# Second parts of plain FFN weight chunks by an accumulating transfer, an earlier read of the plain gate, and tile 4 as a Strassen pair

## The chip, the cores and the metric

The kernel runs on one core of one Trainium2 chip. Its time is the device time of one launch in microseconds (us). Before the change it is 1909.13 us, the median of three runs (1908.13 to 1910.99).

The engines are named as the profile names them: PE is the matrix engine (PEld its weight loads), DVE the vector engine, ACT the scalar engine, POOL the engine that issues software transfers here, and SP the engine that issues the weight loads.

## The reference

One inference step of a two-layer hybrid decoder trunk, in float32. All 520 columns (512 prompt positions and 8 samples) pass through each layer:

```python
x = x + 0.5 * swiglu_ffn(rms_norm(x, p['ffn1_norm']), p['ffn1_wg'], p['ffn1_wu'], p['ffn1_wd'])
h = rms_norm(x, p['mix_norm'])
z = h @ p['w_in']            # retention, sliding-window attention, conv module
...
x = x + y                    # y = concat(three mixers) @ w_out
x = x + 0.5 * swiglu_ffn(rms_norm(x, p['ffn2_norm']), p['ffn2_wg'], p['ffn2_wu'], p['ffn2_wd'])

def swiglu_ffn(x, wg, wu, wd):
    return (jax.nn.silu(x @ wg) * (x @ wu)) @ wd
```

The model width is 1024 and the hidden width of an FFN 2816, that is 22 hidden tiles of 128. There are four FFNs (two per layer) and two mixers. The change touches the FFNs.

## The kernel before

**Precision.** x lies transposed in the core's memory, 128 rows by 520 columns in 8 pieces. Every float32 product is made of three matmuls on float32r operands: each operand is split into a rounded first part and the rest, and first x second, first x first and second x first are summed in PSUM (`mm3`, L342; `product`, L334). For a weight the first part is a cast on ACT (L290, in `split_hi`) and the second part a subtraction on DVE, `wl = w - wh` (L296, in `split_lo`). One matmul works on 128 x 260 columns.

**The weight stream.** All weights come in one order as chunks of 128 x 1024 (512 KB), loaded by SP (L245) into 4 raw buffers. A chunk's buffer is loaded anew when its splits are issued (`done`). The stream is used in one of two ways. A *plain* chunk is split as a whole (one cast and one subtraction of 128 x 1024) and feeds 48 matmuls. Two chunks can instead feed seven *products* of Strassen's kind (a11, s1, s2, a12, s3, s4, a22 in this order), each with a 128 x 512 operand and 12 matmuls; the operands s1, s2 and s4 are sums of weight blocks, made by four DVE additions (L258, L260, L261, L263). So a plain hidden tile takes 2 x 48 = 96 matmuls and a paired one 84, with more work on DVE. The list `PAIRED` names the paired hidden tiles. The hidden results go into three groups (tiles 0 to 7, 8 to 15, 16 to 21); the steps d0, d1 and d2 multiply each group by the down weights, d0 after tile 8, d1 after tile 16 and d2 last. d0 and d1 are paired (`pair_down`), d2 is plain.

**The order of the work.** Each engine runs its instructions in the order in which the program is written. `ahead` splits the weights up to 6 slots ahead of the one in use (a plain chunk counts two slots, a product one). It is called where a chunk or product begins: casts first, then the subtractions, and for a product the next sums. The elementwise work of the tiles before (`gated`, `sum_parts`, `two_parts` and the like) waits in a list from which `advance` takes one step after every product or second k.

**PSUM.** A plain hidden tile has a gate buffer `og` and an up buffer `ou`. After both are complete DVE reads them (`t = og * R`, L443, and `u = ou * R`, L444). A paired tile or pair of down tiles (`seven`) has the buffers `one`, `mid` and the half `c22`. The pool holds four buffers that go round, and so the `mid` of a pair after a plain tile lies where that tile's `og` was: its second product, s1, can begin only after L443. The third product, s2, adds into `c22`, into which ACT first copies the product a11 (L518). A pair that follows a pair waits likewise for the reads of the pair before (`late`, L556 and L557, and `last`, L561, in `pair_hidden`; L542 in `pair_down`). `silu` is L428 on ACT, its product with `u` is L430 on DVE.

Of the kernel before, what the change touches and what calls it, by code (L numbers as in the profile page):

```python
# [10 lines left out]
F32 = mybir.dt.float32  # L11
F32R = mybir.dt.float32r
AF = mybir.ActivationFunctionType
ALU = mybir.AluOpType
# [3 lines left out]
KD = D // 128  # L18
NT = SEQ + NB
HN = NT // 2  # L20
FFN = 2816
NF = FFN // 128

PAIRED = (5, 6, 7, 9, 10, 11, 13, 14, 15, 17, 18, 20, 21)


GROUPS = ((0, 8, True), (8, 16, True), (16, 22, False))
# [82 lines left out]
def ffn_steps():  # L110


    steps = [("hidden", f) for f in range(NF)]
    for n, g in reversed(list(enumerate(GROUPS))):
        steps.insert(min(g[1] + 1, NF), ("down", n))
    return steps


def ffn_tiles(first, gate, up):


    return [(o, k) for k in range(KD) for o in (gate, up)] if first else [(o, k) for o in (gate, up) for k in range(KD)]


def streams():

    w_in = [n for i, n in enumerate(ORDER) if len(n) == 3 and n[:2].isupper() and n not in ORDER[:i]]
    w_out = [(r, int(n[1])) for i, n in enumerate(ORDER) if n[0] in OUT and n[1:].isdigit() and n not in ORDER[:i] for r in OUT[n[0]]]
    return w_in, w_out


MIX_CHUNKS = (len(streams()[0]) * KD + len(streams()[1])) // CT
RAW = 4


@with_exitstack
def step_kernel(ctx: ExitStack, tc: tile.TileContext, io: dict):
    nc = tc.nc

    def pool(name, bufs, **kw):  # L140
        return ctx.enter_context(tc.tile_pool(name=name, bufs=bufs, **kw))

    const = pool("const", 1)
    wraw = pool("wraw", RAW)
    wspl = pool("wspl", 3)
# [11 lines left out]
    R = const.tile([128, NT], F32, name="R")  # L157
# [26 lines left out]
    def v2(t):  # L184
        return t.rearrange("p (a b) -> p a b", a=2)
# [9 lines left out]
    def wt(name, n=NT, dt=F32, bufs=None):  # L195
        return work.tile([128, n], dt, tag="t", name=name)

    def ptile():
        return psum.tile([128, 2, 512], F32, tag="o", name="o")
# [4 lines left out]
    seq, slot = [], [0]  # L204
# [7 lines left out]
    def add_products(n):  # L212
        for _ in range(n):
            for name in PRODUCTS:
                seq.append((name, chunk[0]))
                slot.append(slot[-1] + 1)
            chunk[0] += 2

    chunk = [0]
    for _ in range(DEPTH):  # L220
        for part in range(3):
# [3 lines left out]
            for step, n in ffn_steps():  # L225
                if step == "hidden" and n in PAIRED:
                    add_products(1)
# [4 lines left out]
                else:  # L232
                    add_chunks((GROUPS[n][1] - GROUPS[n][0]) * KD // CT)
    assert chunk[0] == NCH
    raw, done, spl, ready = {}, set(), {}, set()
    at, nxt, loaded, pending = [0, 0], [0], [0], []

    def load(dma=True):

        while loaded[0] < NCH and (loaded[0] < RAW or loaded[0] - RAW in done):  # L240
            i = loaded[0]
            loaded[0] += 1
            raw[i] = wraw.tile([128, CT * 128], F32, tag="w", name="w")
            if dma:
                nc.sync.dma_start(raw[i], io["w"][i])  # L245

    def sums(u):

        if u >= len(seq) or u in ready:
            return  # L250
        ready.add(u)
        name, i = seq[u]
        if name == "chunk":
            return
        load()
        (a21, a11), (a22, a12) = ((raw[j][:, :PC], raw[j][:, PC:]) for j in (i, i + 1))
        if name == "s1":
            nc.vector.tensor_add(Rd[:, 0, :PC], a21, a22)  # L258
        elif name == "s2":
            nc.vector.tensor_sub(a21, a21, a11)  # L260
            nc.vector.tensor_add(Rd[:, 1, :PC], a21, a22)  # L261
        elif name == "s4":
            nc.vector.tensor_sub(Rd[:, 0, :PC], a12, Rd[:, 1, :PC])  # L263

    def source(u):
        name, i = seq[u]
        if name == "chunk":
            return raw[i]
        if name[0] == "a":
            return dict(a11=raw[i][:, PC:], a12=raw[i + 1][:, PC:], a22=raw[i + 1][:, :PC])[name]  # L270
        return raw[i][:, :PC] if name == "s3" else Rd[:, int(name == "s2"), :PC]

    def parts_of(u):

        tag = ("wh", "wl")
        if seq[u][0] == "chunk":
            return tuple(wspl.tile([128, CT * 128], F32R, tag=t, name=t) for t in tag)
        t = tag[slot[u] % 2]
        w = wspl.tile([128, CT * 128], F32R, tag=t, name=t)
        return w[:, :PC], w[:, PC:]  # L280

    def split_hi():

        u = nxt[0]
        if u < len(seq):
            nxt[0] += 1
            load()
            sums(u)
            spl[u] = parts_of(u)
            nc.scalar.copy(spl[u][0], source(u))  # L290
            pending.append(u)

    def split_lo(n=9):
        for u in pending[:n]:
            h, lo = spl[u]
            nc.vector.tensor_sub(lo, source(u), h.bitcast(F32))  # L296
            name, i = seq[u]
            if name in ("chunk", "s3", "a22"):
                done.add(i + (name == "a22"))
                load()  # L300
        del pending[:n]

    def ahead(u):

        old = len(pending)
        while nxt[0] < len(seq) and slot[nxt[0] + 1] - slot[u] <= 6:
            split_hi()
        if seq[u][0] == "chunk":
            split_lo()
        else:  # L310
            split_lo(old)
            sums(nxt[0])
            sums(nxt[0] + 1)

    def next_tile(look=True):
        u, c = at
        if c == 0 and look:
            ahead(u)
        at[:] = (u, c + 1) if c + 1 < CT else (u + 1, 0)
        s = slice(c * 128, (c + 1) * 128)  # L320
        return spl[u][0][:, s], spl[u][1][:, s]
# [17 lines left out]
    def mm3(o, w, vh, vl, first, last):  # L339
        for i, (a, b) in enumerate(((w[0], vl), (w[0], vh), (w[1], vh))):  # L340
            for s in range(2):
                nc.tensor.matmul(  # L342
                    o[:, s, :HN], lhsT=a, rhs=b[:, s * HN : (s + 1) * HN],
                    start=first and i == 0, stop=last and i == 2,
                )
# [20 lines left out]
    def run(parts):  # L366
        for _ in parts:
            pass
# [45 lines left out]
    def advance():  # L414
        while waiting:
            try:
                next(waiting[0])
                return True
            except StopIteration:
                del waiting[0]  # L420

    def flush():
        while advance():
            pass
# [8 lines left out]
    def hidden(norm, first):  # L433

        og, ou = ptile(), ptile()
        for i, (o, k) in enumerate(ffn_tiles(first, og, ou)):
            mm3(o, next_tile(), xh[:, k], xl[:, k], k == 0, k == KD - 1)
            if i % 2:
                advance()
        if first:  # L440
            run(norm)
        t, u = wt("t"), wt("u")
        nc.vector.tensor_mul(v2(t), og[:, :, :HN], v2(R))  # L443
        nc.vector.tensor_mul(v2(u), ou[:, :, :HN], v2(R))  # L444
        return t, u

# [104 lines left out]
    def pair_hidden(blocks):  # L551
        t, u, v = wt("t"), wt("u"), wt("v")[:, :HN]

        def late(c12, c22, m5):
            for d, c in ((t, c12), (u, c22)):
                nc.vector.tensor_add(d[:, HN:], c, v)  # L556
                nc.vector.tensor_mul(d[:, HN:], d[:, HN:], R[:, HN:])  # L557

        def last(one):
            for i, d in enumerate((t, u)):  # L560
                nc.vector.tensor_mul(d[:, :HN], one[:, i, :HN], R[:, :HN])  # L561

        seven(blocks, late, last, lambda m5: nc.scalar.copy(v, m5))
        return t, u

    def ffn(l, name, norm, after):
        hs, even, spare, xs = {n: [] for n in range(len(GROUPS))}, None, [], []
        for step, n in ffn_steps():
            if step == "hidden":
                g = next(i for i, (a, b, _) in enumerate(GROUPS) if a <= n < b)  # L570
                t, u = pair_hidden(xs) if n in PAIRED else hidden(norm, n == 0)
                flush()
                waiting.append(gated(t, u))
                if GROUPS[g][2] and n % 2:
                    waiting.append(pair_blocks(even, u, spare, hs[g]))
                elif GROUPS[g][2] or n == GROUPS[g][0]:
                    even = u
                else:
                    waiting.append(two_parts(u, hs[g]))
                waiting.extend(input_sums(l, name, j, xs) for j in {0: (0,), 1: (1, 2), 2: (3,)}.get(n, ()))  # L580
                continue
# [20 lines left out]
    def mix(l, after):  # L602
# [586 lines left out]
        def chunk_hi():  # L1189
            while True:  # L1190
                split_hi()
                yield

        def chunk_lo():
            while True:
                split_lo(1)
                yield
# [98 lines left out]
def host_arrays(i):  # L1296
# [17 lines left out]
    for t, j in zip(gu, (1, 2)):  # L1314
# [3 lines left out]
        for step, n in ffn_steps():  # L1318
            if step == "hidden":
                g = t[:, n]  # L1320
                if n in PAIRED:

# [96 lines left out]
```

## Time and profile before

| What | Before |
|---|---|
| Median of the runs | 1909.13 us (1908.13 to 1910.99) |
| The profiled execution | 1916.64 us, its span 1914.9 us |
| PE busy | 1843.5 us (96%) |
| DVE busy | 1565.0 us (82%) |
| ACT busy | 991.9 us (52%) |
| POOL busy | 23.3 us (1%) |
| DMA | 189.35 MB, mean 99 GB/s |

The profiled execution is 1.74 us longer than its span, and 7.5 us longer than the median run. A line of the timeline gives the start, the duration, the engine, the line of the kernel, the operation with its operands (out<-in) and its shape; in square brackets stands how long the engine was idle before it and what it waited for. A line of the view of waits gives the engine and line that waited, what it waited for, the sum, the number of times and the longest. A line of the windows gives the stretch, its length, and each engine's busy time with the number of its instructions.

### The profile page before, as it was taken

The numbers are of one execution on the slowest core, as the hardware profiler recorded it, in microseconds if no ns is written. First come the engines' busy times: TensorE is split into PE (matmuls) and PEld (weight loads), VectorE is DVE, ScalarE is ACT, GpSimd is POOL, SyncE is SP. The second block draws the span as 40 slices with busy tenths as digits, with TensorE's granted clock in tenths as the row PEclk, the third lists the DMA queues.
The fourth block names the chain that finished last, engine by engine and source line by source line (L and its number), as shares of the span: only waits on it lengthen the run. The fifth ranks groups of instructions, "written<-read, shape, count | busy, mean of one in ns | idle before, by whom it ended". The sixth has DMA issues, their size and how long they took to land.

```text
span 1914.9 us, 37060 instructions
## 1 busy us (share of the span) xinstructions
PE 1843.5 (96%) x15182; PEld 1818.6 (95%) x15182; DVE 1565.0 (82%) x2691; ACT 991.9 (52%) x1844; POOL 23.3 (1%) x52
## 2 busy tenths in 40 slices
PE   8999999999989999999999999999998999999998
PEld 8999999999989999999999999999998999999998
DVE  8988898688667989888778988976886579889984
ACT  6545555433765645545455455545237555455452
POOL 0000000000100000000000000000000000000000
PEclk9999999999999999999999999999999999999999
DMA  5233333433313222333333332434332132333332
GB/s 181 77 101 100 89 100 111 138 108 114 117 35 97 79 89 89 90 110 98 112 88 90 91 97 89 123 110 127 100 114 102 45 98 69 100 107 92 93 96 89
DMA packets 54170, 189.35 MB, mean 99 GB/s; under 512 B 6272, under 2 KB 7152, under 8 KB 54000
## 3 DMA queue, kind: packets, MB, share of 16 engines
q1 hardware_dynamic: 50784, 177.35, 30.4%
q0 software_dynamic: 3072, 9.53, 1.5%
q8 instruction: 119, 1.95, 0.4%
q14 instruction: 51, 0.42, 0.1%
q10 hardware_dynamic: 144, 0.11, 0.0%
HBM read 179.50 MB, written 7.45 MB: 98 GB/s over the span
## 4 chain that ended last, share of the span: by engine, by line
PE 61%; DVE 26%; ACT 5%; DMA 4%; issue 4%; SPq 0%; DVEq 0%; ACTq 0%; POOL 0%; POOLq 0%
PE o L342 32%; PE o L334 27%; DVE wl L296 5%; DMA w<-in_w 3%; DVE wh L296 3%; DVE m L474 2%; DVE u L430 2%; DVE m L502 1%; DVE w L260 1%; DVE Rd L263 1%; ACT t L428 1%; DVE t L557 1%; DVE t L556 1%; DVE t L561 1%; DVE u L556 1%
## 5 line engine op out<-in xcount | busy, mean ns | idle before, releaser
L342 PE MATMUL o<-xl,wh 128*128 128x260 f32 x1920 | 389.3, 284 | 6.6 <-DVE xl L387 6.1
L342 PE MATMUL o<-xh,wl 128*128 128x260 f32 x1920 | 387.1, 283 | 1.1 <-DVE wl L296 1.1
L342 PE MATMUL o<-xh,wh 128*128 128x260 f32 x1920 | 386.9, 283 | 0.0
L334 PE MATMUL o<-m,wh 128*128 128x260 f32 x2592 | 350.5, 285 | 23.0 <-DVE t L443 11.3
L334 PE MATMUL o<-m,wl 128*128 128x260 f32 x2592 | 351.7, 285 | 21.3 <-DVE t L443 9.8
L290 ACT CAST wh<-w 128x1024 fp32r<-128x1024 f32 (+1 forms) x318 | 261.1, 821 | 200.8 <-PE o L342 127.7
L334 PEld LDWEIGHTS o<-m,wh 128*128 128x128 f32 x2592 | 327.4, 189 | 27.3 <-issue 12.3
L334 PEld LDWEIGHTS o<-m,wl 128*128 128x128 f32 x2592 | 328.5, 190 | 25.7 <-issue 10.8
L342 PEld LDWEIGHTS o<-xl,wh 128*128 128x128 f32 x1920 | 296.9, 189 | 7.9 <-ACT wh L355 6.1
L342 PEld LDWEIGHTS o<-xh,wl 128*128 128x128 f32 x1920 | 296.6, 189 | 1.3 <-DVE wl L296 1.3
L342 PEld LDWEIGHTS o<-xh,wh 128*128 128x128 f32 x1920 | 296.1, 189 | 0.0
L296 DVE TENSOR_TENSOR wl<-w,wh 128x1024 fp32r<-128x1024 f32 x150 | 183.3, 1222 | 36.1 <-ACT wh L290 32.7
L342 PE MATMUL o<-m,wh 128*128 128x260 f32 x1024 | 164.5, 282 | 4.1 <-DVE m L510 4.1
L342 PEld LDWEIGHTS o<-m,wh 128*128 128x128 f32 x1024 | 140.0, 188 | 5.0 <-DVE m L510 5.0
L290 ACT CAST wl<-w 128x512 fp32r<-128x512 f32 x168 | 103.9, 619 | 35.3 <-PE o L334 21.6
L290 ACT CAST wh<-Rd 128x512 fp32r<-128x512 f32 x126 | 78.3, 621 | 82.5 <-PE o L334 34.5
L290 ACT CAST wl<-Rd 128x512 fp32r<-128x512 f32 x126 | 78.3, 622 | 80.2 <-PE o L334 34.4
L428 ACT ACTIVATE t<-t 128x520 f32<-128x520 f32 x88 | 56.1, 638 | 122.8 <-DVE t L561 103.8
L334 PE MATMUL o<-xh,wh 128*128 128x260 f32 x624 | 115.4, 282 | 0.0
L334 PE MATMUL o<-xh,wl 128*128 128x260 f32 x624 | 115.4, 282 | 0.0
L296 DVE TENSOR_TENSOR wl<-w,wl 128x512 fp32r<-128x512 f32 x168 | 114.9, 684 | 0.0
L296 DVE TENSOR_TENSOR wh<-w,wh 128x512 fp32r<-128x512 f32 x168 | 114.9, 684 | 0.0
(216 smaller groups left out, 2660.0 us busy)
## 6 DMA issues: line engine op xcount, KB each, us to landing
w<-in_w SPq DMA_DIRECT2D x318, 512.0 KB, 3.6
out_y<-x SPq DMA_DIRECT2D x8, 260.0 KB, 2.0
m<-in_cm POOLq DMA_DIRECT2D x4, 512.0 KB, 4.3
m<-in_s_ret SPq DMA_DIRECT2D x4, 512.0 KB, 5.2
m<-sc POOLq DMA_DIRECT2D x8, 256.0 KB, 4.6
out_o_rets<-m POOLq DMA_DIRECT2D x4, 512.0 KB, 3.4
x<-in_x SPq DMA_DIRECT2D x3, 520.0 KB, 6.8
w<-in_w SPq DMA_DIRECT2D x4, 256.0 KB, 5.2
```

The costliest lines, as they stand in the source:

```text
L260: nc.vector.tensor_sub(a21, a21, a11)
L263: nc.vector.tensor_sub(Rd[:, 0, :PC], a12, Rd[:, 1, :PC])
L290: nc.scalar.copy(spl[u][0], source(u))
L296: nc.vector.tensor_sub(lo, source(u), h.bitcast(F32))
L334: nc.tensor.matmul(o, lhsT=a[:, s], rhs=b, start=first and j == 0 and i == 0, stop=j == JP - 1 and i == 2, skip_group_check=True,)
L342: nc.tensor.matmul(o[:, s, :HN], lhsT=a, rhs=b[:, s * HN : (s + 1) * HN], start=first and i == 0, stop=last and i == 2,)
L428: nc.scalar.activation(t, t, AF.Silu)
L430: nc.vector.tensor_mul(u, u, t)
L474: nc.vector.tensor_sub(tl[:, c], src, th[:, c].bitcast(F32))
L502: nc.vector.tensor_sub(lo, a, h.bitcast(F32))
L556: nc.vector.tensor_add(d[:, HN:], c, v)
L557: nc.vector.tensor_mul(d[:, HN:], d[:, HN:], R[:, HN:])
```

## The change

It does three things.

1. *Second parts by accumulation.* A plain chunk that is split with at least 72 matmuls ahead of its use (`LEAD`) no longer has its second part from DVE. ACT writes the negated first part into it (new L295, an activation of 128 x 1024 that rounds to float32r), and a transfer issued by POOL (new L296) adds the chunk into it, read a second time from the weights in HBM. The subtraction (now L304) is left out for these chunks. In a run of plain chunks every chunk is split 96 matmuls ahead, behind the products of a pair the second chunk 72 and the first 48; so of the plain chunks after a pair the first keeps its subtraction. In the program this makes 65 transfers and 65 activations. The cast of the first part stays, behind the activation.
2. *The plain gate.* In a plain tile other than an FFN's first, `t = og * R` is written (now L450) right behind the gate's matmuls, that is ahead of the `ahead` of the tile's second chunk, and not behind the up part's matmuls.
3. *Tile 4 is paired.* `PAIRED` has 14 tiles instead of 13, and the FFN's matmuls are 12 fewer.

In the program there are then 77 instead of 150 subtractions of 128 x 1024, while those of 128 x 512 go from 168 to 176 in two forms and from 126 to 132 in two others, and each of the four additions from 84 to 88. SP's loads stay as they are.

```diff
-PAIRED = (5, 6, 7, 9, 10, 11, 13, 14, 15, 17, 18, 20, 21)
+PAIRED = (4, 5, 6, 7, 9, 10, 11, 13, 14, 15, 17, 18, 20, 21)
...
+LEAD = 72
...
-    def split_hi():
+    def split_hi(lead=0):
...
             spl[u] = parts_of(u)
+            if seq[u][0] == "chunk" and lead >= LEAD:
+                added.add(u)
+                nc.scalar.activation(spl[u][1], source(u), AF.Copy, scale=-1.0)
+                nc.gpsimd.dma_start(spl[u][1], io["w"][seq[u][1]], accum_op=ALU.add)
             nc.scalar.copy(spl[u][0], source(u))
             pending.append(u)
...
             h, lo = spl[u]
-            nc.vector.tensor_sub(lo, source(u), h.bitcast(F32))
+            if u not in added:
+                nc.vector.tensor_sub(lo, source(u), h.bitcast(F32))
...
         while nxt[0] < len(seq) and slot[nxt[0] + 1] - slot[u] <= 6:
-            split_hi()
+            split_hi(sum(48 if seq[i][0] == "chunk" else 12 for i in range(u, nxt[0])))
...
             mm3(o, next_tile(), xh[:, k], xl[:, k], k == 0, k == KD - 1)
             if i % 2:
                 advance()
+            if i + 1 == KD and not first:
+                t = wt("t")
+                nc.vector.tensor_mul(v2(t), og[:, :, :HN], v2(R))
         if first:
             run(norm)
-        t, u = wt("t"), wt("u")
-        nc.vector.tensor_mul(v2(t), og[:, :, :HN], v2(R))
+            t = wt("t")
+            nc.vector.tensor_mul(v2(t), og[:, :, :HN], v2(R))
+        u = wt("u")
         nc.vector.tensor_mul(v2(u), ou[:, :, :HN], v2(R))
         return t, u
```

Lines behind the edits move: L443 and L444 are L454 and L456 (L450 for the earlier read), L258 to L263 become L259 to L264, L290 becomes L297, L296 becomes L304, L334 L342, L342 L350, L518 L530, L525 L537, L530 L542, L556 to L561 become L568 to L573.

*Place 1: DVE in the first FFN, from hidden tile 3 to the first sum of the products that follow.* `xg` are sums of the normalised x. Before, tile 4 is still plain and its chunks are subtracted here:

```order
L296 TENSOR_TENSOR wl<-w,wh 128x1024
L430 TENSOR_TENSOR u<-u,t 128x520
L451 TENSOR_TENSOR xg<-xg 128x260
L452 TENSOR_TENSOR xg<-xg 128x260
L453 TENSOR_TENSOR xg<-xg 128x260
L454 TENSOR_TENSOR xg<-xg 128x260
L296 TENSOR_TENSOR wl<-w,wh 128x1024
L474 TENSOR_TENSOR m<-xg,m 128x520 x2
L443 TENSOR_TENSOR t<-o,R 128x520
L444 TENSOR_TENSOR u<-o,R 128x520
L258 TENSOR_TENSOR Rd<-w 128x512
```

The same place in the changed program:

```order
L259 TENSOR_TENSOR Rd<-w 128x512
L304 TENSOR_TENSOR wh<-w,wh 128x512
L304 TENSOR_TENSOR wl<-Rd,wl 128x512
L438 TENSOR_TENSOR u<-u,t 128x520
L463 TENSOR_TENSOR xg<-xg 128x260
L464 TENSOR_TENSOR xg<-xg 128x260
L465 TENSOR_TENSOR xg<-xg 128x260
L466 TENSOR_TENSOR xg<-xg 128x260
L450 TENSOR_TENSOR t<-o,R 128x520
L261 TENSOR_TENSOR w<-w 128x512
L262 TENSOR_TENSOR Rd<-w 128x512
L304 TENSOR_TENSOR wh<-Rd,wh 128x512
```

The sums and splits of tile 4's products stand within tile 3, where two subtractions of 128 x 1024 stood, and the read of the gate stands ahead of the sums for s2.

*Place 2: DVE at hidden tile 8, a plain tile between two pairs.* First the end of tile 7 before the change, where `L556` to `L561` read the pair of tile 7:

```order
L258 TENSOR_TENSOR Rd<-w 128x512
L556 TENSOR_TENSOR t<-o,v 128x260
L557 TENSOR_TENSOR t<-t,R 128x260
L556 TENSOR_TENSOR u<-o,v 128x260
L557 TENSOR_TENSOR u<-u,R 128x260
L296 TENSOR_TENSOR wl<-w,wh 128x1024
L260 TENSOR_TENSOR w<-w 128x512
L261 TENSOR_TENSOR Rd<-w 128x512
```

and after it:

```order
L259 TENSOR_TENSOR Rd<-w 128x512
L568 TENSOR_TENSOR t<-o,v 128x260
L569 TENSOR_TENSOR t<-t,R 128x260
L568 TENSOR_TENSOR u<-o,v 128x260
L569 TENSOR_TENSOR u<-u,R 128x260
L261 TENSOR_TENSOR w<-w 128x512
L262 TENSOR_TENSOR Rd<-w 128x512
```

The subtraction for tile 8's second chunk is gone; that of its first stands a row ahead of both pieces. Then the end of tile 8, before:

```order
L296 TENSOR_TENSOR wl<-Rd,wl 128x512
L296 TENSOR_TENSOR wh<-w,wh 128x512
L474 TENSOR_TENSOR m<-u,m 128x520 x2
L443 TENSOR_TENSOR t<-o,R 128x520
L444 TENSOR_TENSOR u<-o,R 128x520
L430 TENSOR_TENSOR u<-u,t 128x520
L263 TENSOR_TENSOR Rd<-w,Rd 128x512
```

and after:

```order
L450 TENSOR_TENSOR t<-o,R 128x520
L304 TENSOR_TENSOR wh<-Rd,wh 128x512
L304 TENSOR_TENSOR wl<-w,wl 128x512
L486 TENSOR_TENSOR m<-u,m 128x520 x2
L456 TENSOR_TENSOR u<-o,R 128x520
L438 TENSOR_TENSOR u<-u,t 128x520
L264 TENSOR_TENSOR Rd<-w,Rd 128x512
```

The read of the gate moved up by three rows; the row that makes s4's operand (L263, now L264) still stands last.

*Place 3: ACT at the end of tile 7*, where tile 8's two chunks are cast (`wh<-w 128x1024`). Before:

```order
L290 CAST wh<-w 128x1024
L530 COPY o<-o 128x260
L290 CAST wh<-w 128x1024
L290 CAST wl<-w 128x512
L290 CAST wh<-Rd 128x512
```

and after, with tile 8's second chunk negated ahead of its cast:

```order
L297 CAST wh<-w 128x1024
L542 COPY o<-o 128x260
L295 ACTIVATE wl<-w 128x1024
L297 CAST wh<-w 128x1024
L297 CAST wh<-w 128x512
```

One activation of 128 x 1024 more stands on ACT in front of the second cast.

More of the change, by code (lines that the diff above doesn't have):

```diff
@@ L234, in step_kernel @@
     assert chunk[0] == NCH
-    raw, done, spl, ready = {}, set(), {}, set()
+    raw, done, spl, ready, added = {}, set(), {}, set(), set()
     at, nxt, loaded, pending = [0, 0], [0], [0], []
```

## The prediction

> **What bounds the kernel now.** I read the busy times first, then the chain that ended last, then PE's waits, then the stretches in which these lie.
>
> ```profile
> PE 1843.5 (96%) x15182; PEld 1818.6 (95%) x15182; DVE 1565.0 (82%) x2691; ACT 991.9 (52%) x1844; POOL 23.3 (1%) x52
> ...
> PE 61%; DVE 26%; ACT 5%; DMA 4%; issue 4%; SPq 0%; DVEq 0%; ACTq 0%; POOL 0%; POOLq 0%
> ```
>
> PE is busy 96%, but the chain runs over DVE for 26% of the span: at many places DVE decides when PE's operands are there.
>
> ```profile
> PE o L334 <- DVE t L443: 21.0, 12, 2.5
> PE o L334 <- DVE u L556: 12.2, 12, 1.0
> PE o L334 <- ACT o L518: 11.0, 12, 1.2
> ...
> PE o L342 <- DVE m L510: 4.1, 4, 1.1
> ```
>
> Twelve is three per FFN: behind the plain tiles 8, 12 and 16 the next pair's s1 waits 1.75 us on average (21.0 / 12) for the read of the gate; L556 costs 1.0 in front of tiles 7, 11 and 15. The wait for ACT's copy L518 stands behind tiles 8 and 16, and seldom elsewhere.
>
> The stretch that decides is that from the end of tile 2 to the end of tile 8. In two FFNs (columns: stretch, length, then each engine's busy time with its instructions):
>
> ```profile
> 629.10:700.30 71.20, 68.34 (x564) 67.62 (x562) 64.84 (x119) 37.72 (x73) 0.00 (x0) 1.00 0.26 75
> 995.80:1067.20 71.40, 68.52 (x564) 67.61 (x562) 64.85 (x119) 37.62 (x73) 0.00 (x0) 1.00 0.25 75
> ```
>
> DVE works 64.84 of 71.20 us and idles 6.36. These rows of the first of the two tell what the idle time is:
>
> ```profile
> 629.09 0.70 DVE L444 TENSOR_TENSOR u<-o,R 128x520 f32<-128x520 f32 x1
> ...
> 633.02 1.31 DVE L474 TENSOR_TENSOR m<-xg,m 128x520 fp32r<-128x520 f32 x2 [0.28 <-ACT m L470]
> 634.50 1.23 DVE L296 TENSOR_TENSOR wl<-w,wh 128x1024 fp32r<-128x1024 f32 x1 [0.17 <-ACT wh L290]
> ...
> 638.02 1.22 DVE L296 TENSOR_TENSOR wl<-w,wh 128x1024 fp32r<-128x1024 f32 x1
> ...
> 649.43 0.69 DVE L296 TENSOR_TENSOR wl<-Rd,wl 128x512 fp32r<-128x512 f32 x1 [0.74 <-ACT wl L290]
> ...
> 679.39 0.69 DVE L296 TENSOR_TENSOR wl<-w,wl 128x512 fp32r<-128x512 f32 x1
> ...
> 684.84 0.69 DVE L258 TENSOR_TENSOR Rd<-w 128x512 f32<-128x512 f32 x1 [3.43 <-DMA w<-in_w]
> ```
>
> 3.43 us go to a load whose raw buffer comes free only with the subtraction at 679.39. Whatever makes DVE later makes this load and its wait later too, so it absorbs nothing. Three round trips to ACT are 0.28 + 0.17 + 0.74 = 1.19; the rest are gaps of tenths between instructions. So from tile 2 to d0 DVE is a chain almost without slack.
>
> **Part A: tile 4 as a pair.** It adds seven subtractions and four sums of 128 x 512, the reads of a pair (`late`, `last`), and takes away the two reads of a plain tile and three subtractions of 128 x 1024: tile 4's own two (634.50, 638.02) and, by the accumulation, that of tile 8's second chunk (687.05). Prices are distances from start to start on the busy DVE:
>
> ```profile
> 651.87 0.69 DVE L443 TENSOR_TENSOR t<-o,R 128x520 f32<-128x520 f32 x1
> ...
> 653.08 0.68 DVE L263 TENSOR_TENSOR Rd<-w,Rd 128x512 f32<-128x512 f32 x1
> ...
> 655.23 0.69 DVE L258 TENSOR_TENSOR Rd<-w 128x512 f32<-128x512 f32 x1
> ...
> 660.84 0.43 DVE L556 TENSOR_TENSOR t<-o,v 128x260 f32<-128x260 f32 x1
> ...
> 662.45 0.68 DVE L296 TENSOR_TENSOR wl<-w,wl 128x512 fp32r<-128x512 f32 x1
> 663.05 0.42 DVE L561 TENSOR_TENSOR t<-o,R 128x260 f32<-128x260 f32 x1
> ...
> 663.73 0.68 DVE L296 TENSOR_TENSOR wh<-w,wh 128x512 fp32r<-128x512 f32 x1
> ...
> 687.05 1.22 DVE L296 TENSOR_TENSOR wl<-w,wh 128x1024 fp32r<-128x1024 f32 x1
> 688.18 0.68 DVE L260 TENSOR_TENSOR w<-w 128x512 f32<-128x512 f32 x1
> ```
>
> Nine instructions of 128 x 512 or like it take 660.84 - 655.23 = 5.61, 0.62 each: eleven cost 6.85. `late` costs 662.45 - 660.84 = 1.61 and `last` 0.68; the two plain reads give back 653.08 - 651.87 = 1.21. A subtraction of 128 x 1024 gives back 1.13, three 3.40. Sum: 6.85 + 1.61 + 0.68 - 1.21 - 3.40 = +4.53 us on DVE's chain. The 0.17 idle ahead of a removed subtraction goes with it: +4.3, which I take. If all round trips to ACT are absorbed (1.19) it is +3.3. If two more like that of 0.74 come with tile 4's seven products, +5.9.
>
> PE gets 12 matmuls less:
>
> ```profile
> 683.66 0.40 PE L342 MATMUL o<-xl,wh 128*128 128x260 f32 x2
> ...
> 695.19 1.59 PE L334 MATMUL o<-m,wh 128*128 128x260 f32 x12
> 698.37 1.67 PE L334 MATMUL o<-m,wl 128*128 128x260 f32 x12 [1.58 <-DVE t L443]
> 701.27 1.71 PE L334 MATMUL o<-m,wh 128*128 128x260 f32 x12 [1.23 <-ACT o L518]
> ```
>
> Tile 8's 96 matmuls last 11.53 us, 0.12 each, so 1.44 is saved. It becomes wait: the stretch ends when d0's s2 starts (701.27), and that hangs on DVE. PE's new waits should stand at tiles 4 to 7, where the products' operands are now late.
>
> **Part B: the earlier read of the gate.** What stands behind the wait for L443 is the next wait:
>
> ```profile
> 699.55 0.69 DVE L263 TENSOR_TENSOR Rd<-w,Rd 128x512 f32<-128x512 f32 x1
> ...
> 700.32 0.62 ACT L290 CAST wl<-Rd 128x512 fp32r<-128x512 f32 x1 [0.91 <-DVE Rd L263]
> 700.85 0.37 ACT L518 COPY o<-o 128x260 f32<-128x260 f32 x1
> ```
>
> s2 needs ACT's copy L518; on ACT it is queued behind the cast of s4's operand, and that behind L263 on DVE. The gate's read only moves up three rows within the same DVE chain; L263 still stands last. So s1 starts earlier, and s2 waits longer. What shortens the chain is the subtraction left out, 1.13, at the junctions behind tiles 12 and 16: 2 x 1.13 = -2.3 (tile 8's is in A). If neither shortens, 0; if the whole wait for L443 goes, a rival below.
>
> **Part C: the transfers beside the loads.** The accumulations for tiles 8, 12 and 16 are issued just when the load is under way for which L258 waits:
>
> ```profile
> DVE Rd L258 <- DMA w<-in_w: 47.4, 16, 4.3
> ...
> DMA to landing us min/median/max: 3.5/4.1/4.6
> ```
>
> The second line is that of the four loads from 676 to 692 us. From median to longest are 0.5 us; between 0 and 0.55 per junction I take 0.2, as at 26% DMA share (the window's row) there is room: +0.6 per FFN. [...]
>
> **Part D: are the accumulations in time?** The trace has none. The nearest rows are POOL's transfers of the same size, and ACT's casts and activations:
>
> ```profile
> w<-in_w SPq DMA_DIRECT2D x318, 512.0 KB, 3.6
> ...
> m<-in_cm POOLq DMA_DIRECT2D x4, 512.0 KB, 4.3
> ...
> out_o_rets<-m POOLq DMA_DIRECT2D x4, 512.0 KB, 3.4
> ```
>
> ```profile
> L290 ACT CAST wh<-w 128x1024 fp32r<-128x1024 f32 x150 | 157.1, 1047 | 166.0 <-PE o L342 115.6 <-issue 44.1 <-ACT sq L392 3.8
> ...
> L485 ACT ACTIVATE xg<-x,par 128x520 f32<-128x520 f32 x32 | 21.5, 719 | 0.0
> ```
>
> An accumulation must read the weights (at least 4.3) and may read and write the target one after the other (4.3 + 4.3 + 3.4 = 12.0); I take 4.3 + 3.4 = 7.7 as the likely most. A chunk split 72 matmuls ahead has 72 x 0.12 = 8.6 us, and 0.5 more, as only the fifth matmul of a chunk asks for the second part; less some 1.7 for the wait for ACT's copy and the negation itself (0.7 and 1.05, the cast's time; an activation of 128 x 520 takes 0.72): 7.4. A chunk split 96 ahead has 2.9 more. So the cost is 0, or 0.3 at the five chunks with 72 ahead (tiles 8, 12, 16, 19 and d2): 1.5 per FFN at most by that. ACT, busy 37.72 of 71.20, hides its negations; where they stand ahead of a cast that DVE waits for, that subtraction is gone. The subtractions left out elsewhere (tiles 0 to 3, d2, the mixers' borders) stood beside a PE that did not wait for them: 0.
>
> **Sum** per FFN: 4.3 - 2.3 + 0.6 + 0 = +2.6; four FFNs +10.4. The profiled execution would go from 1916.6 to 1927; it is 7.5 above the median of the runs, and against that median the time is 1909.1 + 10.4 = **1919 us**.
>
> **The rivals.**
>
> *1. The look-ahead absorbs tile 4.* Splits run six slots ahead, and DVE's idle time before tile 3 grows by the subtractions left out there; if DVE enters the stretch ahead, the 12 matmuls are a gain and three junctions each lose 1.13: -1.44 - 3.4 = -4.8 per FFN, -19: 1890; half of it, 1900. It decides from the point where DVE's load of 64.84 + 4.5 fits into 71.2 - 1.4 = 69.8 without the wait of 3.43. For it: the load itself would just fit. Against: that wait is tied to DVE's own instruction, and the order on DVE is fixed, with the sums of tile 4 inside tile 3. 0.25.
>
> *2. The accumulations land late.* At 10 us, the middle between 7.7 and 12.0, they are 2.6 late: PE stops 2.6 at tile 19 and d2 and, where later waits shrink in turn (by 1.9, 0.9 and 1.9), 0.7, 1.7 and 0.7 at tiles 8, 12 and 16: 8.3 per FFN, +33; with the rest 1952. For it: every one goes through POOL, whose transfer takes 0.7 longer than SP's, beside a DVE that hardly rests. Against: the budget of 7.4 is well above 4.3. 0.12. [...]
>
> *3. The gate's read is worth its whole wait.* If L518 does not take over, three junctions give 1.75 each instead of B's 2.3: 4.3 - 5.25 + 0.6 = -0.35 per FFN, 1908. Against it the row at 701.27, where L518 already comes 1.23 late. 0.13.
>
> **How the numbers follow.** Forecast 0.50, rivals 0.25, 0.12, 0.13. The forecast's own range: 3.3 - 2.3 + 0 = +1.0 per FFN to 5.9 - 2.3 + 1.65 + 1.5 = +6.75, that is 1913 to 1936. The whole range reaches into rival 1's half gain and leaves out its full gain and rival 2: 1898 to 1938. What this kernel's measurement can tell from no change is 0.2%, 3.8 us. Faster: rival 1 (0.25), a little of rival 3 and of the forecast (0.04): 0.29. Same: most of rival 3 and the forecast's edge: 0.13. Slower: the rest of the forecast (0.46) and rival 2: 0.58.
>
> **What would show it.** Right: in the stretch from tile 2 to tile 8 DVE's busy time up by about 4 and the stretch longer, not shorter; PE waits at tiles 4 to 7 that were not there; no wait for L454 or L450, and longer ones for the copy L530 behind tiles 8, 12 and 16. Rival 1: the stretch 1.4 or more shorter, PE without new waits at tiles 4 to 6. Rival 2: PE waits for the transfer into `wl` at tiles 19 and d2, and issue to landing above 7.4. Rival 3: no longer wait for L530. The forecast is wrong if these waits sum to less than what PE saves.

## The result and the profile after

The changed kernel takes 1935.97 us (median of four runs, 1931.93 to 1938.67) against 1910.06 us before on the same chip: 1.0131 times as long, with an interval of 1.0104 to 1.0158, or about 25 us. That is slower, as forecast, within the stated range of 1898 to 1938, and 17 us above the 1919 that were predicted. The profiled execution took 1938.67 us.

The page of the changed kernel, first the span and the busy times, then (of the part on DMA issues) the two kinds of weight transfers, with the size and the median time from issue to landing:

```profile
span 1936.9 us, 37199 instructions
...
PE 1849.4 (95%) x15134; PEld 1821.2 (94%) x15134; DVE 1513.4 (78%) x2678; ACT 1065.5 (55%) x1945; POOL 79.8 (4%) x117
...
w<-in_w SPq DMA_DIRECT2D x318, 512.0 KB, 3.8
wl<-in_w POOLq DMA_DIRECT2D x65, 512.0 KB, 7.9
```

DVE has 52 us less to do, and PE has 48 matmuls less and is busy 6 us longer. An accumulation takes 7.9 us to land, and the view of line L296 has the spread of the 65:

```profile
DMA to landing us min/median/max: 5.6/7.9/11.8
```

What PE waited for in the changed kernel:

```profile
PE o L350 <- DMA wl<-in_w: 26.6, 23, 2.5
PE o L342 <- DVE u L568: 16.1, 12, 2.0
PE o L342 <- ACT o L530: 13.8, 12, 2.2
...
PE o L342 <- DVE m L486: 5.7, 4, 1.4
```

The 21.0 us of waits for the read of the gate are gone. In their place stand 26.6 us for accumulations that are not there in time, at 23 places; 12.5 of them behind the matmuls of tiles 8, 12 and 16. The stretch from the end of tile 2 to s4's operand of d0 in the second FFN, which before took 71.20 us with DVE busy 64.84, now reads:

```profile
637.70:714.60 76.90, 69.77 (x545) 68.54 (x545) 69.22 (x132) 42.49 (x84) 0.87 (x1) 0.96 0.29 82
```

DVE has 4.4 us more to do there, the stretch is 5.7 us longer, and the granted clock (the third number from the end) is 0.96. The forecast had 4.5 and 4.3. Most of the difference stands at the end of tile 8, where PE first waits for a late accumulation, and DVE then for PE:

```profile
706.85 0.51 PE L350 MATMUL o<-xh,wl 128*128 128x260 f32 x2 [0.81 <-DMA wl<-in_w]
...
712.44 0.70 DVE L456 TENSOR_TENSOR u<-o,R 128x520 f32<-128x520 f32 x1 [0.88 <-PE o L350]
```

The new waits of PE lie where they were forecast, at tile 4 (s1 and s2) and tile 7 (s1):

```profile
652.83 0.62 PE L342 MATMUL o<-m,wl 128*128 128x260 f32 x3 [1.45 <-DVE m L486]
655.62 2.38 PE L342 MATMUL o<-m,wh 128*128 128x260 f32 x12 [2.17 <-ACT o L530]
...
689.38 2.05 PE L342 MATMUL o<-m,wh 128*128 128x260 f32 x12 [2.03 <-DVE u L568]
```

The durations 2.38 and 2.05 for 12 matmuls, which take 1.6 to 1.7 elsewhere, come from a lower clock: the first reaches into the window below with a granted clock of 0.50, the second into another, with 0.50 too, from 690.53 on.

```profile
656.39:659.80 3.41, 3.41 (x18) 3.41 (x18) 3.38 (x7) 2.75 (x8) 0.00 (x0) 0.50 0.60 189
```

### The profile page after: what moved, and what is told of

It reads as the page before. It is cut to its first block, busy times and chain, and to the rows that moved or that the text cites. A ratio compares the mean times of both kernels' runs of the same rounds, so it can differ in the third digit from the quotient of the medians.

```text
span 1936.9 us, 37199 instructions
## 1 busy us (share of the span) xinstructions
PE 1849.4 (95%) x15134; PEld 1821.2 (94%) x15134; DVE 1513.4 (78%) x2678; ACT 1065.5 (55%) x1945; POOL 79.8 (4%) x117
## 3 DMA queue, kind: packets, MB, share of 16 engines
q0 software_dynamic: 12432, 43.61, 11.8%
## 5 line engine op out<-in xcount | busy, mean ns | idle before, releaser
L342 PE MATMUL o<-m,wh 128*128 128x260 f32 x2688 | 367.1, 286 | 25.9 <-ACT o L530 13.8
L350 PE MATMUL o<-xh,wl 128*128 128x260 f32 x1792 | 363.8, 285 | 18.2 <-DMA wl<-in_w 18.2
L342 PE MATMUL o<-m,wl 128*128 128x260 f32 x2688 | 364.1, 284 | 12.5 <-DVE m L486 5.7
L342 PEld LDWEIGHTS o<-m,wh 128*128 128x128 f32 x2688 | 342.5, 191 | 30.5 <-ACT o L530 16.3
L350 PE MATMUL o<-xl,wh 128*128 128x260 f32 x1792 | 364.1, 284 | 6.9 <-DVE xl L395 5.7
L350 PE MATMUL o<-xh,wh 128*128 128x260 f32 x1792 | 361.6, 283 | 0.0
L297 ACT CAST wh<-w 128x512 fp32r<-128x512 f32 (+1 forms) x318 | 255.7, 808 | 183.0 <-PE o L350 129.8
L342 PEld LDWEIGHTS o<-m,wl 128*128 128x128 f32 x2688 | 340.1, 190 | 16.5 <-DVE m L486 6.5
L350 PEld LDWEIGHTS o<-xh,wl 128*128 128x128 f32 x1792 | 277.3, 189 | 21.9 <-DMA wl<-in_w 21.7
L350 PEld LDWEIGHTS o<-xl,wh 128*128 128x128 f32 x1792 | 277.8, 189 | 8.1 <-ACT wh L363 5.7
L350 PEld LDWEIGHTS o<-xh,wh 128*128 128x128 f32 x1792 | 277.0, 189 | 0.0
L350 PE MATMUL o<-m,wh 128*128 128x260 f32 x1024 | 165.7, 284 | 0.0
L350 PEld LDWEIGHTS o<-m,wh 128*128 128x128 f32 x1024 | 141.2, 190 | 0.4
L342 PE MATMUL o<-xh,wl 128*128 128x260 f32 x672 | 126.6, 286 | 0.0
L297 ACT CAST wl<-Rd 128x512 fp32r<-128x512 f32 x132 | 82.1, 622 | 80.3 <-PE o L342 32.7
L297 ACT CAST wl<-w 128x512 fp32r<-128x512 f32 x176 | 108.9, 619 | 28.6 <-PE o L342 20.4
L342 PE MATMUL o<-xh,wh 128*128 128x260 f32 x672 | 124.3, 282 | 0.0
L297 ACT CAST wh<-Rd 128x512 fp32r<-128x512 f32 x132 | 82.0, 621 | 75.5 <-PE o L342 32.1
L296 POOL DMA_DIRECT2D wl<-in_w x65 | 56.5, 870 | 1563.5 <-PE o L342 814.9
L304 DVE TENSOR_TENSOR wh<-w,wh 128x512 fp32r<-128x512 f32 x176 | 120.4, 684 | 0.0
L304 DVE TENSOR_TENSOR wl<-w,wl 128x512 fp32r<-128x512 f32 x176 | 120.4, 684 | 0.0
L350 PE MATMUL o<-m,wl 128*128 128x260 f32 x512 | 103.8, 284 | 8.4 <-DMA wl<-in_w 8.4
```

Source lines behind the costliest of these rows:

```text
L296: nc.gpsimd.dma_start(spl[u][1], io["w"][seq[u][1]], accum_op=ALU.add)
L342: nc.tensor.matmul(o, lhsT=a[:, s], rhs=b, start=first and j == 0 and i == 0, stop=j == JP - 1 and i == 2, skip_group_check=True,)
L350: nc.tensor.matmul(o[:, s, :HN], lhsT=a, rhs=b[:, s * HN : (s + 1) * HN], start=first and i == 0, stop=last and i == 2,)
```

## The experiments

Each was run against the kernel before, whose median was 1910 to 1913 us in these groups; ratios are to that. Differences in us are those of medians, where nothing else is said. The code shown is cut to the lines that matter.

### The three parts by themselves

Tile 4 alone: `PAIRED = (4, 5, ...)` in the kernel before.

> The kernel before with tile 4 paired and nothing else. Chain theory: the stretch from tile 2 to d0 is a DVE chain, and of part A only the subtraction for tile 8's second chunk (1.13) stays, so +5.4 per FFN, +22, about 1932, with PE waits of 1 to 2 us at tiles 4 to 7. Look-ahead theory: tile 4's work fits into DVE's idle time and PE keeps its 12 matmuls, -1.4 per FFN, about 1904.

Measured: 1929.9 us, 1.0105 (1.0092 to 1.0118), +20. That is the size that the chain theory gave.

The early read alone, the kernel before with this edit:

```diff
+            if i + 1 == KD and not first:
+                t = wt("t")
+                nc.vector.tensor_mul(v2(t), og[:, :, :HN], v2(R))
```

> The kernel before with the plain gate read early and nothing else. Chain theory: the waits for the gate's read vanish but the copy ahead of s2 comes no earlier, so its wait grows by the same amount: 0 (1906 to 1914), copy waits up from 11 to about 30 us. Whole-wait theory: 21 us are saved, about 1889.

Measured: 1919.6 us, 1.0053 (1.0041 to 1.0066): +9.3. Neither theory had that. PE's waits do what the chain theory says:

```profile
PE o L334 <- ACT o L522: 32.2, 13, 3.0
```

32.2 is about the sum of the two waits of before, 21.0 for the gate and 11.0 for the copy. So the waits together have not grown, and yet 9 us are lost. The rows behind tile 16 of the second FFN show how. Before:

```profile
832.74 1.67 PE L334 MATMUL o<-m,wl 128*128 128x260 f32 x12 [1.58 <-DVE t L443]
835.64 1.71 PE L334 MATMUL o<-m,wh 128*128 128x260 f32 x12 [1.23 <-ACT o L518]
```

With the early read, and behind it three windows of 3.40 us from there on (the third number from the end is the granted clock):

```profile
837.27 2.97 PE L334 MATMUL o<-m,wh 128*128 128x260 f32 x12 [2.89 <-ACT o L522]
840.04 1.76 PE L334 MATMUL o<-m,wl 128*128 128x260 f32 x12
...
833.60:837.00 3.40, 0.78 (x7) 0.58 (x5) 3.16 (x7) 0.67 (x2) 0.00 (x0) 1.00 0.00 0
837.00:840.40 3.40, 3.13 (x14) 3.13 (x15) 3.33 (x6) 1.41 (x4) 0.00 (x0) 0.50 0.61 172
840.40:843.80 3.40, 3.40 (x31) 3.40 (x29) 2.49 (x5) 1.92 (x5) 0.00 (x0) 1.00 0.43 141
```

Two waits of 1.58 and 1.23 us with 12 matmuls between them became one of 2.89, and after it PE's clock is halved for 3.4 us: 14 matmuls fit in, 31 afterwards. What stands behind the wait is work of PE's own, so the slower matmuls cost up to 1.7 us each time (half of 3.41, an estimate). In the FFNs of this run there are eight such periods, all behind tiles 8, 12 and 16; in the profiled run of the kernel before three, one of them of double length.

The transfers: the changed kernel without the line of the accumulating DMA, so that these second parts are missing from its result.

> The changed kernel without the 65 accumulating transfers; the negated first parts stay, so the second parts are left out of the result, and every other instruction is there. Prices the transfers. If each wait for a transfer (26.6 us) is lost time: about 1909. Chain theory: at tiles 12 and 16 and partly at 8 the DVE chain would have held PE anyway, so only the waits at tiles 1, 19 and d2 and a part at 8 count, -15 to -19: about 1919. If the transfers also slow the loads by part C, 2 to 3 us below that.

Measured: 1916.3 us, 1.0038 (1.0026 to 1.0051), 18 to 20 below the changed kernel (by the ratios and by the medians). The chain theory held (1919; the 3 us below it are what part C would give, but the scatter is as large), and with it its reading that not all of the 26.6 us were lost time. PE's wait for the copy grows instead (the copy is L529 in this kernel; it was 13.8 us in the changed kernel):

```profile
PE o L341 <- ACT o L529: 22.1, 16, 2.5
```

At tiles 12 and 16 one takes the place of the other: late accumulations (8.0 us over the four FFNs) and copy (4.0) are 12.0 us in the changed kernel, and the copy alone is 12.1 here. At tile 8 it is not so. The wait for the copy there is 0.3 to 0.4 us in each FFN in both kernels, and the accumulations' 4.5 us came on top. In the second FFN:

```profile
704.95 1.70 PE L341 MATMUL o<-m,wh 128*128 128x260 f32 x12 [0.32 <-ACT o L529]
```

```profile
715.57 1.70 PE L342 MATMUL o<-m,wh 128*128 128x260 f32 x12 [0.30 <-ACT o L530]
```

The first row is of the kernel without the transfers, the second of the changed one.

All but tile 4: `PAIRED = (5, ...)` in the changed kernel.

> The changed kernel with tile 4 plain again (13 paired tiles), so accumulation and the early read alone. If tile 4 costs on DVE's chain what it cost alone, less the subtraction of tile 8's second chunk that is left out here (19.6 - 4 x 1.13 = 15): about 1921. If the accumulations' lateness is what the change costs and tile 4 is harmless: 1932 or more.

Measured: 1913.1 us, 1.0014 (1.0000 to 1.0028). That is 8 below the 1921 that was expected for a cost on DVE's chain. The 4.5 for tile 8's second chunk should not have been taken off, because this kernel and the changed one both leave that subtraction out; 1916 would have been the number. So tile 4 costs about 23 us in the changed kernel, 3 more than alone, and accumulation and early read together come out even.

### The clock

A test of the cause: let PE work while it waits. 12 matmuls on a pair's first block, with their sums in a PSUM half that is overwritten later, behind the pair's s1, only after tiles 8, 12 and 16. The edit that does it, the second form to be run (the function `fill` and the passing on of `busy` are left out here):

```diff
         product("s1", m5, blocks, True)
+        if busy:
+            fill(c12, blocks)
```

A first form wrote its sums into another half, `c21`, and by that came to stand behind the wait instead of ahead of it:

```diff
+        if busy:
+            fill(c21, blocks)
         product("s2", c22, blocks, False)
```

> The kernel before with the early read, and 12 matmuls on data at hand whose sums nobody reads, put ahead of the s2 that follows a plain tile (12 places), so that PE is busy for 1.4 us of the wait there. Clock theory: the early read costs 9.3 us because the two waits become one of 2.8 us, after which the granted clock is 0.5 for 3.41 us; with the fill those windows after tiles 8, 12 and 16 go and the time is that of before, 1910 (1906 to 1913). If the early read costs by its place in DVE's order: 1919 or more, as the fill changes nothing there.

Measured: 1938.3 us, 1.0153 (1.0132 to 1.0173). The expectation failed, by my edit: c21 lies in the buffer that ACT's copy reads, so the fill waited for the copy like s2 itself:

```profile
707.84 1.70 PE L521 MATMUL o<-m 128*128 128x260 f32 x12 [2.98 <-ACT o L531]
```

It left the wait as it was and lengthened the path by 12 x 1.44 = 17 us, most of the 19 us that it lies above 1919.6. It says nothing on the clock; the second form does.

> The kernel before with the early read, and the 12 matmuls ahead of the wait of s2: in a half of a PSUM buffer that nobody else uses yet, right behind s1, so they wait for nothing (in the first fill they waited for ACT's copy too, and 12 x 1.44 us were added behind the wait). Clock theory: PE idles less than 1.7 us in any 3.41 us there, the half-clock windows after tiles 8, 12 and 16 are gone, and the time is that of before: 1908 to 1913. If the early read costs by something else: 1919, and up to 1937 if the fill lengthens the path.

Measured: 1908.4 us, 0.9977 (0.9961 to 0.9994), 11 us below the early read alone, with more work on PE. The wait of s2 is then 1.5 us and no half-clock window is left in this run's FFNs:

```profile
826.02 1.60 PE L521 MATMUL o<-m 128*128 128x260 f32 x12
829.15 1.70 PE L334 MATMUL o<-m,wh 128*128 128x260 f32 x12 [1.54 <-ACT o L531]
```

So the early read cost its 9 us by the clock. In itself it is worth little: this time is 3 us below the kernel before, and part of that may be that kernel's own half-clock periods. The fill without the early read was not run.

The same question where the accumulations with 72 matmuls ahead are left out, `LEAD = 96`, with tile 4 paired:

> The changed kernel with accumulations only where 96 matmuls lie ahead, so that tiles 8, 12, 16, 19 and d2's second chunk have their subtraction back. Lateness theory: most waits for transfers go, about 1915. Chain theory: the waits at tile 19 and d2 go (-12), but the subtractions at tiles 8, 12 and 16 are back on the chain (3 x 1.13 x 4 = +13.6), less what the transfers had cost at tile 8 (2 to 4): about 1934, no gain.

Measured: 1950.2 us, 1.0210 (1.0195 to 1.0225). That is 14 us above the changed kernel, where the chain theory had no change and the other a gain. With the fill of the second form:

> The changed kernel with accumulations only where 96 matmuls lie ahead, and the same 12 matmuls ahead of s2's wait. Clock theory: of the 14 us that lead96 lay above the changed kernel 10 to 14 come from its windows at half clock after tiles 8, 12 and 16 (7 of 18), so 1936 to 1941. If the subtractions on the chain cost them: 1950.

Measured: 1935.1 us, 1.0129 (1.0113 to 1.0145). So the 14 us above the changed kernel were the clock's. The spans and mean granted clocks, first without and then with the fill:

```profile
core 0: 1944.0 us, clock 0.981
```

```profile
core 0: 1933.3 us, clock 0.989
```

So the chain theory's count was right (no gain from leaving out the late transfers), and a late accumulation at tiles 8, 12 and 16 has one good side: it cuts PE's wait into two pieces.

And tile 4: does it cost by DVE's chain, or by the clock that halves in tiles 4 to 7? The changed kernel with the fill ahead of the waits of tile 4 and 7, where `busy` holds 1 and 2 for tile 4, and 1 for tile 7:

```diff
         product("a11", c11, blocks, True)
+        if 1 in busy:
+            fill(c21, blocks)
...
         product("s1", m5, blocks, True)
+        if 2 in busy:
+            fill(c12, blocks)
```

> The changed kernel with 12 matmuls on data at hand, whose sums nobody reads, ahead of the waits of tile 4 (s1 and s2) and of tile 7 (s1), so that PE idles less than 1.7 us in any 3.41 us there. It tells whether tile 4 costs by DVE's chain or by the granted clock. Chain theory: the eight half-clock windows in tiles 4 to 7 vanish, but DVE sets the pace there, so the time stays, 1931 to 1938. Clock theory: eight times up to 1.7 us come back, about 1922.

Measured: 1931.2 us, 1.0101 (1.0082 to 1.0119). The interval overlaps that of the changed kernel, and the time lies far above 1922, though the half-clock periods of tiles 4 to 7 (seven in the changed kernel's trace) are all gone. The stretch of tiles 3 to 6 in the second FFN, of the changed kernel and then with the fill:

```profile
638.40:692.30 53.90, 47.58 (x369) 46.56 (x368) 50.97 (x98) 30.92 (x64) 0.00 (x0) 0.95 0.22 65
```

```profile
636.80:690.70 53.90, 50.61 (x412) 49.37 (x411) 50.97 (x99) 30.86 (x64) 0.00 (x0) 1.00 0.22 65
```

43 matmuls more (36 of them the fill) and a full clock in place of 0.95, and the same 53.90 us, with DVE busy 50.97 in both. There the chain on DVE sets the pace and PE's clock is hidden.

### Only the accumulations that lie on the chain

13 paired tiles, and an accumulation only for the second chunks of tiles 8, 12 and 16, 12 transfers instead of 65 (`tile_of` gives the tile that a second chunk belongs to):

```diff
-            if seq[u][0] == "chunk" and lead >= LEAD:
+            if tile_of.get(u) in (8, 12, 16) and lead >= LEAD:
```

> 13 paired tiles, the early read, and accumulation only for the second chunks of tiles 8, 12 and 16 (12 transfers). Chain theory: each leaves a subtraction of 1.13 out of the DVE chain that sets the next pair's s2, and the transfer's lateness (0.4 to 1.8) lies within that wait: -13.6 against the kernel before, 1897, if no new windows at half clock come; with eight as in the early read alone, about 1905. If the lateness is lost time: 1910 or more.

Measured: 1897.0 us, 0.9936 (0.9920 to 0.9952), -14 us (-12 by the ratio). That is the number of the chain theory, and there are no half-clock windows in the FFNs.

> The same with the 12 idle matmuls ahead of the s2 that follows tiles 8, 12 and 16. Clock theory: no half-clock windows there, 1895 to 1899. If the remaining wait is shorter than 1.4 us the fill itself costs up to 12 x 0.5 us: 1903.

Measured: 1912.4 us, 1.0017 (1.0005 to 1.0030), neither of the numbers expected. This has the first form of the fill, behind the wait, and there was no window to remove: it shows the fill's own cost, 15 us or 12 x 1.3.

> 13 paired tiles and accumulation only for the second chunks of tiles 8, 12 and 16, with the gate read in its old place. If the early read is worth nothing (the copy ahead of s2 decides): as junc_early, 1897. If it saves a part once a subtraction has left the chain: 1900 to 1905.

Measured: 1894.4 us, 0.9920 (0.9907 to 0.9934), the fastest of all, 0.8% below the kernel before. The early read adds nothing here either. The remaining waits at these places (L351 has the matmuls of plain chunks, L527 is the copy):

```profile
PE o L351 <- DMA wl<-in_w: 11.7, 12, 2.0
PE o L343 <- ACT o L527: 6.2, 11, 1.2
```

17.9 us instead of the 32.0 of before, 14 us less: 12 subtractions of 1.13 are 13.6.

## Why the prediction was right, and by how much it missed

The sum can be set against differences of runs, in us over four FFNs (by medians):

| Term | Predicted | Measured | From |
|---|---|---|---|
| Tile 4 as a pair (A without tile 8's subtraction) | 4 x (4.3 + 1.13) = +22 | +23, and +20 alone | changed kernel less 13 paired tiles; tile 4 alone |
| Subtractions off the chain at tiles 8, 12, 16 (B, and the rest of A) | 12 x -1.13 = -14 | -14 | 12 accumulations only, with the early read |
| Early read of the gate | 0 | +9 alone, -3 with the fill | the early read alone, gate_fill2 |
| The other accumulations (C and D) | +2 | +16 | 13 paired tiles less 12 accumulations only |
| Sum | +10 | +25 | |

The early read is not in the measured sum by itself: the kernels of the other rows have it. The three rows that make up the sum give +25 by construction, as each is the difference between two neighbouring kernels; by the ratios they are +22, -12 and +15. They do not part the terms cleanly. The kernel with 13 paired tiles has 73 accumulations, eight of them for tile 4, with 5.5 us of waits at tile 4 that the changed kernel does not have.

That the time lies in the stated range is in part luck. D's bound was 1.5 us per FFN, and the other accumulations cost about 4. The room for it came from the bounds of A and C, which were hardly needed: the forecast's own range ended at 1936, just where the time is.

**Part A** stood, in size and in place. DVE's work in the stretch rose by 4.4 us (forecast 4.5), and the saved matmuls became wait. That the stretch grew by 5.7 and not 4.3 is in the main the late accumulation at its end. The fill at tiles 4 and 7 showed that PE's time does not matter there.

**Part B** stood: the copy L518 takes over from the gate's read, and only the subtraction counts. What it did not see is that the same sum of waits in another arrangement changes the clock. In the changed kernel itself this hardly shows behind tiles 8, 12 and 16, because the late accumulations split the wait again; seven of the eight windows in its FFNs lie in tiles 4 to 7, under the DVE chain, and the eighth in d2 of the third FFN. One forecast sign did not come: the copy's wait behind tiles 8, 12 and 16 should have grown from 11.0 us, and it is 5.2, as the late accumulations came first. The other 8.7 of the 13.8 stand at tile 4.

**Part D is the step that failed**: "So the cost is 0". Its budget was right: at the five chunks per FFN with 72 matmuls ahead, landing less wait comes to 7.4 to 7.6 us, against the 7.4 of the prediction. The landing time was the term that was mis-sized. It took 7.7 us as the likely most; these twenty took 7.7 to 9.3, 8.5 on average. So all of them were late, by 0.2 to 1.8 us, 1.0 on average. At tiles 12 and 16 this lay within a wait that was there anyway. At tile 8 (4.5 us over the four FFNs), at tile 19 (3.2) and in d2 (8.4) it did not, and at tile 1 of the first FFN another 2.5 were lost. The d2 waits include a chunk with 96 matmuls ahead in the first and the third FFN, beside three other accumulations and four loads. The waits in d2 of the first FFN:

```profile
353.87 0.51 PE L350 MATMUL o<-m,wl 128*128 128x260 f32 x2 [1.78 <-DMA wl<-in_w]
...
361.54 0.50 PE L350 MATMUL o<-m,wl 128*128 128x260 f32 x2 [1.67 <-DMA wl<-in_w]
```

And d2 as a window, from the start of its first matmul to the start of the next step, in the changed kernel, in that without the transfers and in the kernel before:

```profile
345.54:384.13 38.59, 35.14 (x291) 34.62 (x290) 16.39 (x25) 21.61 (x28) 6.55 (x11) 1.00 0.85 205
```

```profile
343.14:377.76 34.62, 34.62 (x291) 34.52 (x289) 16.39 (x25) 21.67 (x28) 0.00 (x0) 1.00 0.38 114
```

```profile
341.63:377.40 35.77, 34.75 (x291) 34.54 (x289) 24.52 (x32) 15.95 (x22) 0.00 (x0) 1.00 0.38 115
```

The DMA share is 0.85 with the transfers and 0.38 without. Over the four FFNs d2 is 11.6 us longer with them than without; in the third FFN a half-clock window behind the waits adds to it.

The last two rows show a smaller miss of D. It took the subtractions left out in d2 to be worth 0, but the kernel before waits 1.0 us there in each FFN, the 4.1 us for L510 that the prediction shows:

```profile
346.42 0.76 PE L342 MATMUL o<-m,wh 128*128 128x260 f32 x4 [1.02 <-DVE m L510]
```

That wait is gone in the changed kernel and in that without the transfers, and back with `LEAD = 96`, which gives the subtraction of d2's second chunk back. From the first read L556 to L510 DVE takes 5.26 us in the kernel before (340.40 to 345.66), and 4.14 where that subtraction is left out. So the accumulations saved 4 us in d2, and lost more by being late.

**Part C** was small, as forecast. The waits of DVE for loads did not grow against the kernel before, they fell from 47.4 us to:

```profile
DVE Rd L259 <- DMA w<-in_w: 41.4, 16, 3.8
```

Without the transfers, but with tile 4 paired, they are 40.0 us. So by these two traces the transfers added 1.4 us, where 2.4 were forecast; the 1.65 per FFN at the upper end of the forecast's range, three times 0.55, was an estimate, and these traces show 0.35 per FFN. The larger slowing shows on the accumulations. The last two of the launch, with no load under way, took 5.6 and 5.7 us (the one before them 7.0, beside two others); with two or three loads it was 6.8 to 9.3, with four loads and three other accumulations 10.7 to 11.8. No run changes the loads alone, and a longer transfer also meets more of them, so that the loads are the cause is not shown.

**The rivals.** The look-ahead did not absorb tile 4 (1). The accumulations landed late (2), with both of its signs, waits at tile 19 and d2 and landing times above 7.4, but by less than priced: 1.0 us on average and not 2.6. About half of that rival's loss of 33 us, on top of the forecast, makes up the miss. Of its reason, POOL's transfers beside a DVE that hardly rests, the trace shows little: the first packet of an accumulation with no other before it started 1.6 to 2.6 us after its issue (once, at the start, 3.1), against 1.1 to 1.4 for POOL's other transfers, so most of the 7.9 is transfer. That the early read is worth its whole wait (3) is refuted by the early read alone and by the fill.

What stays open: whether the 3 to 6 us by which tile 4 costs more in the changed kernel, or by which the fill made it cheaper, are more than scatter; and why an accumulation takes 5.6 us even with no load beside it, and how much of its time is reading its target, which no run separates.

## What to carry to other kernels

Move work off an engine only where a wait ends on it: with 13 paired tiles, 12 accumulations gave the whole gain of 14 us, and the other 61 cost 16. A transfer that takes the place of an instruction needs its landing time under load (here 8.5 us on average, where 7.7 had been reckoned with), not its typical one, ahead of its use. And before two waits are merged by starting something earlier, look at the granted clock, which fell to 0.50 for 3.4 us behind a merged wait of 2.89 us here: it may be cheaper to leave them apart, or to let PE do matmuls ahead of the wait whose results nobody reads.

## What the runs showed of the hardware that was not expected

The granted clock went down though PE had idled for only a part of the time ahead. In the traces of the kernel before and of the changed one it is 0.50 for 3.41 or 6.83 us at a time (but for the period that the end of the launch cuts off). In the FFNs there are three such periods before the change and eight after it. In the 3.41 us ahead of each PE was idle for 1.84 to 2.18 us in the kernel before and for 1.74 to 2.78 us in the changed one, never for the whole of it. The 1.7 us under which the fills were to keep PE's idle time lies just below the least of these.

The waits of 1.58 and 1.23 us behind tile 16 in the second FFN of the kernel before left the clock at 1.00 (831.53 to 838.35); the one of 2.89 us that the early read made of them was followed by 0.50. The kernel before also has cases close to each other: four stretches of 3.41 us behind its plain tiles have 1.73 to 1.84 us of idle time, and only the one with 1.84 was followed by half clock; its other two periods stand behind single waits of 2.1 and 2.4 us at tile 12. What else decides there, no run shows.

Idle time is not the whole measure. In the mixers of these two traces, four half-clock periods, two in each, follow 3.4 us in which PE shows no idle time at all. The first of them in the kernel before (0.50 from 493.61 on) stands behind this window, which holds 32 matmuls, 28 of them with only 2 columns:

```profile
490.20:493.60 3.40, 3.40 (x32) 3.40 (x32) 3.05 (x4) 3.37 (x5) 0.00 (x0) 1.00 0.37 105
```
